# Two channel tiles of a 31-tap depthwise convolution: from VectorE/GpSimd taps to column-grouped fp32 products on TensorE

## The chip, the core and the metric

The kernel runs on one core of a Trainium2 chip. The metric is device time in microseconds of one execution; three executions of the kernel before took 2930.77, 2932.99 and 2934.18 us, median 2932.99 us. The engines are called PE (TensorE matmul), PEld (its weight loads), DVE (VectorE), ACT (ScalarE), POOL (GpSimd) and SP (SyncE, which here only issues DMAs). All arithmetic is fp32; the large products split each operand into a high part `wh`/`hh` and a low part `wl`/`hl` in the faster fp32r format and add three products.

## The reference

Two trunk layers over 512 latent tokens and 256 context tokens of width 1024. Each layer is half-step SwiGLU, a token mixer, half-step SwiGLU. The change lies in the mixer of the even (first) layer, which runs two head groups side by side: multi-head latent attention with 8 heads, and a Conformer convolution module over 512 channels:

```python
def conv_module(u, prm):
    u = u + prm["conv_glu_b"]
    a, g = jnp.split(u, 2, axis=-1)
    y = a * jax.nn.sigmoid(g)
    y = depthwise_conv(y, prm["conv_dw_w"], width 31, zero padding 15 on both sides) + prm["conv_dw_b"]
    y = layer_norm(y, prm["conv_ln_g"], prm["conv_ln_b"])
    return jax.nn.silu(y)
```

Latent and context tokens are convolved separately. The results of both head groups are concatenated and multiplied by `w_out`.

## The kernel before, in words

Features lie on the 128 partitions and tokens along the free axis, so the 512 convolution channels are four tiles c = 0..3 of 128 channels. `conv_unit(c)` makes one tile's gated input: two products of the mixer's input with 128 columns of weights (8 row tiles, three split products each, for 512 and 256 tokens), a sigmoid on ACT, and two DVE instructions that add the bias, multiply and write `yb[c]`: one row of 813 numbers per channel, with zeros ahead, between and behind latent and context. Before each product, `unit` loads 128 x 1024 weights (SP queue), rounds them on ACT (`wh`, line 210) and takes the rest on DVE (`wl`, line 211); PE needs both, and the load buffer is free again only when DVE has made `wl`.

`conv_taps(c, lo, hi, pool)` applies taps to a row of 783 outputs `cv[c]`. Tap 0 is one ACT instruction (line 768). On DVE another tap is one fused multiply-add (line 774). On POOL it is two instructions, a product into a scratch row and an addition (lines 771 and 772). The division of the 4 x 31 taps is:

- tiles 0 and 2: 2 ACT taps and 60 DVE taps, handed over ahead of the attention;
- tile 1: 1 ACT tap and 30 POOL taps, and of tile 3 taps 0 to 7 (1 ACT, 7 POOL), handed over at the same place;
- tile 3, taps 8 to 11: POOL, inside the attention; taps 12 to 30: 19 DVE taps inside the attention, one per query tile at some of them.

`even_mixer` hands its work over in this order: first low-rank product `wA`; `conv_unit` 0 to 3; second low-rank product `wB` (a `sweep` over six token tiles); transposes of both low-rank results (`lora_t`, line 899, ACT high part in line 901, DVE low part through line 199); keys and values (`up_tile`), their norms; queries, their norms and rotation; the taps; attention (`flow`); the layer norm of the convolution (`conv_ln`); its activation (`conv_act`); the output product `mix_out`.

What sets the order: a planner goes through the handed-over instructions with a cost estimate of its own and writes down a fixed order for each engine, taking what is ready, earlier-handed first. So the taps, handed over late, fill holes that the planner sees on DVE and POOL from the moment `yb[c]` exists. On the chip each engine then runs its list strictly in that order. The attention is different: its instructions are pinned, that is, kept in the order written. `flow` has 48 items (8 heads x 6 query tiles); an item may carry extras, among them single taps (`TAPT`, `PTAPT`), quarter transposes of the next head's operands, and one of the 14 steps of `conv_ln`. Those steps begin at item `LN0` = 25 or later, when no tap is left.

Buffers: areas A0 to E3 are shared by name. A0 to A3 hold the residual stream until the mixer's input is made (it is saved to HBM and read back by `mix_out`), A3 then serves as POOL's scratch row, A0 to A2 later hold the keys. PSUM has three pairs of banks handed out in turn by `pd()` (names `pa`, `pb`), and two single banks (`p`).

Of the kernel before, what the change touches and what calls it, by code (L numbers as in the profile page):

```python
# [31 lines left out]
TAPS3 = 12  # L32
TAPS3E = 8
LN0 = 25
# [17 lines left out]
DT = (0, 0, 0, 0, 0, 0, 99, 0)  # L52
PT = (0, 0, 0, 0, 0, 0, 99, 0)
TAPT = (0, 2, 4, 5)
PTAPT = (0, 2, 4)
# [38 lines left out]
class Kern:  # L94
# [57 lines left out]
    # one of twenty areas A0..E3; a new tile takes over the area from the one before  # L152
# [4 lines left out]
    # n rows of width w, so many per area  # L157
# [23 lines left out]
    # two banks, from the three pairs in turn  # L181
# [52 lines left out]
    # r = 1 / sqrt(ss * inv_n + eps), one Newton step after the table's square root  # L234
# [19 lines left out]
    # per-token 1/rms of the accumulated squares, the same on all partitions  # L254
# [36 lines left out]
    # four column chunks of 256 go to four column groups; a last product with a  # L291
    # selector brings both vectors to the feature layout
# [29 lines left out]
    # the same on the vector engine: half of the columns, two row tiles per unit  # L322
    def mod_dve(self):
        nc = self.nc
        self.mod_fin(1)
        L, m = self.mq[0]
        nv = self.mv(L, m)
        hh, kk = self.mk // 4, self.mk % 4
        u = self.mt().rearrange("p (a n) -> p a n", a=2)
        c0 = m * 1024 + hh * 512  # L330
        nc.sync.dma_start(u, self.I[f"modw{L}"][kk * 256:(kk + 1) * 256, c0:c0 + 512].rearrange("(a p) n -> p a n", p=128))
        if kk == 0:
            self.macc = [self.t768()[:, :512] for _ in range(nv)]
        for a in range(2):
            for v in range(nv):
                sc = self.sT[:, kk * 2 + a, v:v + 1]
                if kk == 0 and a == 0:
                    nc.vector.tensor_scalar(self.macc[v], u[:, a, :], sc, None, op0=ALU.mult)
                else:
                    self.stt(self.macc[v], u[:, a, :], sc, self.macc[v], ALU.mult, ALU.add)  # L340
        self.mk += 1
        if kk < 3:
            return
        if hh:
            self.mk = 0
            self.mq.pop(0)
        acc = self.macc

        r = slice(0, 64 * nv)
        st = {}  # L350

        # sums over the rows, one column group per vector and quarter
        def sums():
            p = self.p1()[:, 0:256]
            for v in range(nv):
                for q in range(2):
                    g = 64 * v + 32 * q
                    nc.tensor.matmul(p[g:g + 32, :], self.ones[:, 0:32], acc[v][:, q * 256:(q + 1) * 256], start=True, stop=True, tile_position=(0, g))  # L358
# [13 lines left out]

        self.mfin += [sums, fin]
# [6 lines left out]
    # vectors that a part is needed for  # L380
# [3 lines left out]
    # one step in the background; no half is begun that the slots left can't end  # L384
# [36 lines left out]
    # operand of an FFN: x * g * (1 + scale), split; the rms factor comes after the product  # L421
# [23 lines left out]
    # the shift's columns on their own, both parts side by side  # L445
# [131 lines left out]
    # modulated input of a mixer, split, in slots B and C  # L577
# [15 lines left out]
    # tokens x columns product, k outer; returns one PSUM area per token tile  # L593
# [26 lines left out]
    # natural-layout product with resident split operands (lora up-projections)  # L620
# [8 lines left out]
    # keep an engine's order as traced  # L629
# [66 lines left out]
    # values of two query tiles side by side in the columns of the array  # L696
# [14 lines left out]
    # the two halves to the rows of head h  # L711
# [14 lines left out]
    def rope_tables(self, gname, cname, sname, n, h):  # L726
        # g1*cos, g2*sin, g1*sin, g2*cos
# [31 lines left out]
    # taps lo..hi of one channel tile; latent and context share one row with zeros between  # L759
    def conv_taps(self, c, lo, hi, pool, pin=lambda i: i):  # L760
# [4 lines left out]
        for w in range(lo, hi):  # L765
            yw = y[:, w:w + CW]
            if w == 0:
                pin(nc.scalar.activation(cv, yw, AF.Identity, bias=self.col("dwb")[:, c:c + 1], scale=dw[:, 0:1]))
            elif pool:
                t = self.ctmp or self.mt()[:, :CW]  # L770
                pin(nc.gpsimd.tensor_scalar(t, yw, dw[:, w:w + 1], 1.0, op0=ALU.mult, op1=ALU.mult))
                pin(nc.gpsimd.tensor_tensor(cv, cv, t, op=ALU.add))
            else:
                pin(nc.vector.scalar_tensor_tensor(cv, yw, dw[:, w:w + 1], cv, op0=ALU.mult, op1=ALU.add))  # L774

    # layer norm over the channels, in steps; what a step returns follows one step later
# [57 lines left out]
    def even_mixer(self):  # L834
# [7 lines left out]
        self.ctmp = self.area("A3")[:, :CW]  # L842
# [4 lines left out]
        # lora parts  # L847
# [12 lines left out]
        tq = [(c, w) for c in (0, 2) for w in range(31)]  # L860
        pq = [(1, w) for w in range(31)] + [(3, w) for w in range(TAPS3E)]
        p3 = [(3, w) for w in range(TAPS3E, TAPS3)]
        d3 = [(3, w) for w in range(TAPS3, 31)]

        def taps(i):
            for q, n in ((pq, PT[i]), (tq, DT[i])):
                for c, w in q[:n]:
                    self.conv_taps(c, w, w + 1, q is pq)
                del q[:n]

        self.conv_unit(0)
        self.conv_unit(1)
        taps(0)
        self.conv_unit(2)
        taps(1)
        self.conv_unit(3)
        taps(2)
# [9 lines left out]
        taps(3)  # L887
        taps(4)
        # transposed lora activations, gains applied on the way
# [14 lines left out]
        # keys and values  # L904
# [25 lines left out]
        taps(5)  # L930
        # shared rotary part of the keys
# [13 lines left out]
        # a quarter of head h's transposed operands: three token tiles of K or of Q  # L945
# [19 lines left out]
        # queries  # L965
# [37 lines left out]
        taps(6)  # L1003
        tq += d3
        # attention
        self.ctmp = None
# [18 lines left out]
        def mk(h, t):  # L1025
# [22 lines left out]
            if t in TAPT and tq and (tq[0][0] != 3 or not p3):  # L1048
                c, w = tq.pop(0)
                ex.append(lambda: self.conv_taps(c, w, w + 1, False, self.pin))  # L1050
            if t in PTAPT and p3:
                w3 = p3.pop(0)[1]
                ex.append(lambda: self.conv_taps(3, w3, w3 + 1, True, self.pin))
# [4 lines left out]
            if h * 6 + t >= LN0 and ln and not tq and not p3:  # L1058
# [7 lines left out]
        for c, w in tq:  # L1066
            self.conv_taps(c, w, w + 1, False)
# [8 lines left out]
    def rope_q(self, x, T, nh):  # L1076
        # x [128, nh, 64] of one latent token tile, in place
# [12 lines left out]
    def odd_mixer(self):  # L1090
# [19 lines left out]
        # grouped-query part  # L1110
# [22 lines left out]
        # neighbourhood part  # L1133
# [18 lines left out]
        # split keys and queries, on the way to their transposes  # L1152
# [35 lines left out]
        # GQA keys [kh;kh], [kl;kl] and queries [qh;ql], once half of the sweep is done  # L1188
# [24 lines left out]
        # attention  # L1213
# [3 lines left out]
        # heads of the neighbourhood part: [kh;kl], [qh;qh], [ql;ql], two sets in turn  # L1217
# [165 lines left out]
    def build(self):  # L1383
# [20 lines left out]
        for L in range(2):  # L1404
# [15 lines left out]
            # the latent half of the norm and of the mixer's input runs under the context's products  # L1420
# [56 lines left out]
def _units(w):  # L1477
    # [1024, 128 * n] -> [n, 128, 8 * 128]: unit n holds its columns for the 8 row tiles
# [19 lines left out]
def _rows(w):  # L1498
    # [1024, n] -> [128, 8 * n]
# [3 lines left out]
def _pp(v):  # L1503
    # [128 * n] -> [128, n]
# [18 lines left out]
def _perm(a):  # L1523
    # latent tokens: row-major to column-major on the grid
# [25 lines left out]
def layout(a):  # L1550
# [42 lines left out]
    put("dwb", _pp(a["l0_conv_dw_b"]))  # L1593
    put("lng", _pp(a["l0_conv_ln_g"]))
# [58 lines left out]
```

## Time and profile before

| | |
|---|---|
| three runs | 2930.77, 2932.99, 2934.18 us |
| profiled execution | span 2929.3 us from first to last instruction; no time of its own is given beside the span, which is 3.7 us under the runs' median |
| busy over the span | PE 2812.6, PEld 2436.2, DVE 1708.6, ACT 855.1, POOL 460.0 us |
| granted TensorE clock | mean 0.982 |
| first and last DVE tap (line 774) | starts at 675.1 and 944.9 us, 79 of them |
| POOL taps (lines 771, 772) | 41 pairs, from 690.4 to about 879 us |
| first attention score product (line 1035) | 864.1 us |
| first `mix_out` product | 991.8 us |

How to read it: times of the trace count from the span's start. A wait is idle time of an engine, with the instruction that ended it. A row of the timeline gives start, length, engine, line, operation and operands; "x7" means seven instructions in a row. PE instructions are recorded with overlapping, modelled ends, so the distance between starts is the better measure of PE's pace. An fp32 product appears as two PE instructions, an fp32r product as one. The stage table gives, for stretches of the span, each engine's busy time, PE's granted clock (1.00 is full speed) and DMA use.

### The profile page before, as it was taken

What the parts mean: (1) busy time and instruction counts of PE and PEld (TensorE: products, weight loads), DVE (VectorE), ACT (ScalarE), POOL (GpSimd) and SP (SyncE); (2) the same over time, 40 slices, a digit from 0 to 9 for tenths busy, and PEclk for the clock granted to TensorE, in tenths of its full rate; (3) what the DMA queues carried; (4) which work ended last, traced back from release to release, by engine and by line L of the source; (5) the groups of instructions that cost most, each with busy time, mean ns of one, the idle gap of its engine ahead of it and who ended that gap; (6) DMA issues with size and microseconds to landing.
All of it is one profiled execution on the core that took longest, in us unless ns stands there. A gap on an engine that the chain in (4) does not pass through costs nothing.

```text
span 2929.3 us, 41724 instructions
## 1 busy us (share of the span) xinstructions
PE 2812.6 (96%) x17276; PEld 2436.2 (83%) x17276; DVE 1708.6 (58%) x2709; ACT 855.1 (29%) x1281; POOL 460.0 (16%) x435
## 2 busy tenths in 40 slices
PE   8999999998479899999999999999999999999999
PEld 5888888887467788888888888888888888898998
DVE  2665666688987676656545533333336779643443
ACT  3211212242156522112122221121224257332221
POOL 1000000035943330000000300000011256300000
PEclk9999999999789999999999999999999999999999
DMA  6433343431010223333433111112124200222232
GB/s 219 129 122 124 120 139 116 127 124 46 31 42 2 72 87 120 118 116 116 140 126 102 59 63 66 59 60 69 59 86 126 65 12 30 87 94 94 88 97 90
DMA packets 93740, 266.62 MB, mean 91 GB/s; under 512 B 8816, under 2 KB 9968, under 8 KB 93552
## 3 DMA queue, kind: packets, MB, share of 16 engines
q1 hardware_dynamic: 86512, 247.89, 26.6%
q10 hardware_dynamic: 5376, 10.83, 1.2%
q0 software_dynamic: 1664, 5.24, 0.5%
q8 instruction: 136, 2.23, 0.3%
q14 instruction: 52, 0.43, 0.0%
HBM read 255.80 MB, written 7.34 MB: 90 GB/s over the span
## 4 chain that ended last, share of the span: by engine, by line
PE 88%; DVE 7%; ACT 2%; issue 1%; DMA 1%; POOL 1%; ACTq 0%; SPq 0%; DVEq 0%; POOLq 0%
PE pa L190 53%; PE pb L190 26%; DVE D L774 3%; PE p L706 2%; PE pb L659 2%; DVE wl L211 1%; PE pa L1035 1%; PE pa L1263 1%; PE p L358 1%; ACT t L661 1%; PE p L193 0%; DMA r<-in_modw 0%; DVE sm L672 0%; PE p L279 0%; DVE C L199 0%
## 5 line engine op out<-in xcount | busy, mean ns | idle before, releaser
L210 ACT CAST wh<-r 128x1024 fp32r<-128x1024 f32 (+3 forms) x334 | 340.6, 1020 | 1517.8 <-PE pa L190 776.1
L190 PE MATMUL pa<-B,wh 128*128 128x512 f32 (+1 forms) x1984 | 492.8, 330 | 10.9 <-DVE D L199 8.6
L190 PE MATMUL pa<-B,wl 128*128 128x512 f32 (+1 forms) x1984 | 487.5, 327 | 0.0
L190 PE MATMUL pa<-C,wh 128*128 128x512 f32 (+1 forms) x1984 | 487.0, 327 | 0.3 <-DVE C L428 0.3
L211 DVE TENSOR_TENSOR wl<-r,wh 128x1024 fp32r<-128x1024 f32 (+3 forms) x334 | 410.7, 1230 | 39.8 <-ACT wh L210 31.0
L190 PEld LDWEIGHTS pa<-B,wh 128*128 128x128 f32 x1984 | 308.6, 190 | 50.9 <-issue 15.8
L190 PEld LDWEIGHTS pa<-C,wh 128*128 128x128 f32 x1984 | 307.9, 190 | 35.7 <-issue 0.7
L190 PEld LDWEIGHTS pa<-B,wl 128*128 128x128 f32 x1984 | 307.7, 190 | 34.1 <-issue 0.5
L199 DVE SCALAR_TENSOR_TENSOR t<-m,sT,t 128x512 f32<-128x512 f32 x392 | 275.7, 752 | 3.9 <-DMA m<-in_modw 2.8
L190 PE MATMUL pa<-E,wh 128*128 128x512 f32 (+1 forms) x919 | 257.7, 347 | 1.3 <-POOL E L215 1.3
L517 DVE COPY sm<-pa 128x2 f32<-128x2 f32 x116 | 18.4, 159 | 395.7 <-PE pa L190 395.1
L190 PE MATMUL pb<-B,wh 128*128 128x512 f32 (+1 forms) x960 | 236.5, 328 | 0.0
L190 PE MATMUL pb<-B,wl 128*128 128x512 f32 (+1 forms) x960 | 234.0, 325 | 0.0
L190 PE MATMUL pb<-C,wh 128*128 128x512 f32 (+1 forms) x960 | 233.5, 324 | 0.0
L190 PE MATMUL pa<-D,wh 128*128 128x512 f32 (+1 forms) x777 | 204.4, 339 | 0.1
L190 PE MATMUL pa<-D,wl 128*128 128x256 f32 (+1 forms) x737 | 196.3, 339 | 0.0
L1416 POOL DMA_DIRECT2D xs<-A x24 | 13.5, 562 | 1089.0 <-DVE A L199 1087.3
L190 PEld LDWEIGHTS pa<-E,wh 128*128 128x128 f32 x919 | 148.2, 188 | 24.3 <-POOL E L215 1.7
L190 PEld LDWEIGHTS pb<-B,wh 128*128 128x128 f32 x960 | 148.6, 189 | 19.6 <-issue 4.2
L190 PEld LDWEIGHTS pb<-C,wh 128*128 128x128 f32 x960 | 148.2, 189 | 16.2
L190 PEld LDWEIGHTS pb<-B,wl 128*128 128x128 f32 x960 | 148.2, 189 | 15.8
L199 DVE SCALAR_TENSOR_TENSOR A<-pa,hg,A 128x256 f32<-128x256 f32 (+1 forms) x95 | 54.9, 614 | 172.1 <-PE pa L190 172.0
(329 smaller groups left out, 4470.3 us busy)
## 6 DMA issues: line engine op xcount, KB each, us to landing
m<-in_modw SPq DMA_DIRECT2D x140, 512.0 KB, 3.7
r<-in_win0a SPq DMA_DIRECT2D x44, 512.0 KB, 4.2
r<-in_win0b SPq DMA_DIRECT2D x44, 512.0 KB, 3.5
r<-in_win1a SPq DMA_DIRECT2D x44, 512.0 KB, 3.4
r<-in_win1b SPq DMA_DIRECT2D x44, 512.0 KB, 3.4
r<-in_wodd SPq DMA_DIRECT2D x18, 512.0 KB, 3.7
r<-in_wout0a SPq DMA_DIRECT2D x20, 448.0 KB, 3.5
r<-in_wout1a SPq DMA_DIRECT2D x20, 448.0 KB, 3.4
```

The costliest lines, as they stand in the source:

```text
L190: self.nc.tensor.matmul(out, l.bitcast(F32R), r.bitcast(F32R), start=st, stop=sp)
L199: self.nc.vector.scalar_tensor_tensor(o, a, s, b, op0=op0, op1=op1)
L210: pin(self.nc.scalar.copy(hi, r))
L211: pin(self.nc.vector.tensor_tensor(lo, r, hi.bitcast(F32), op=ALU.subtract))
L358: nc.tensor.matmul(p[g:g + 32, :], self.ones[:, 0:32], acc[v][:, q * 256:(q + 1) * 256], start=True, stop=True, tile_position=(0, g))
L517: nc.vector.tensor_copy(w2[:, o:o + 2], p[:, so:so + 2])
L659: pin(nc.tensor.transpose(pt[:, ks], P[:, ks], self.col("ident")))
L661: pin(nc.scalar.copy(PT[:, :m], pt[:, :m]))
L706: self.pin(self.nc.tensor.matmul(self.po[i * 64:(i + 1) * 64, col:col + 128], v, self.PTs[i][:, kt * 128:(kt + 1) * 128], start=(kt == 0), ...
L774: pin(nc.vector.scalar_tensor_tensor(cv, yw, dw[:, w:w + 1], cv, op0=ALU.mult, op1=ALU.add))
L1035: self.pin(nc.tensor.matmul(s[:, o:o + b - a], q[:, ts].bitcast(F32R), k[:, a:b].bitcast(F32R), start=j == 0, stop=j == 2))
L1263: self.pin(nc.tensor.matmul(s[:, a:b], q.bitcast(F32R), k[:, a:b].bitcast(F32R), start=j == 0, stop=j == 1))
```

## The change

Tiles 1 and 3 are computed on TensorE. `conv_fan` copies the finished row `yb[c]` to four operands Y[0..3], one for each 32 channels: Y[g] has the 32 channels four times on its 128 partitions, copy s shifted by s tokens. That is 16 SBUF-to-SBUF DMAs of 32 partitions x about 811 fp32 numbers (about 104 KB) per tile, alternately on the SP and the ACT queue. `conv_mm` then multiplies Y[g] by a 128 x 32 weight block with the taps 4j..4j+3 on its diagonals, for j = 0..7 (tap 31 is zero), once for the 512 latent and once for the 256 context outputs. The four g go to four column groups of the array (`tile_position`), plain fp32; that makes 64 products per tile. Two ACT instructions add the bias and write `cv[c]`. The weight blocks are laid out on the host (`wdw`, 512 KB per tile), loaded by SP. Y lies in areas A0 to A3, whose last columns are zeroed by four small POOL instructions.

Tiles 0 and 2 keep their 2 ACT and 60 DVE taps, handed over at the same place. POOL has no tap, the attention has none, and the 14 layer-norm steps begin at item 8 instead of 25 or later. Comments are removed too, which shifts line numbers by a few.

```diff
-TAPS3 = 12
-TAPS3E = 8
-LN0 = 25
+PEC = (1, 3)
+LN0 = 8
...
+    def conv_fan(self, c, Y):
+        nc = self.nc
+        y = self.yb[c]
+        n = CW + 28
+        for s in range(4):
+            for g in range(4):
+                m = min(n, YW - s)
+                e = (nc.sync, nc.scalar)[(s + g) % 2]
+                e.dma_start(Y[g][32 * s:32 * s + 32, 0:m], y[32 * g:32 * g + 32, s:s + m])
+
+    def conv_mm(self, c, Y):
+        nc = self.nc
+        wd = self.mt()
+        nc.sync.dma_start(wd, self.I["wdw"][PEC.index(c)])
+        p = self.pd()
+        for j in range(8):
+            for a, b, o in LNREG:
+                for g in range(4):
+                    nc.tensor.matmul(p[32 * g:32 * g + 32, a:b], wd[:, j * 128 + 32 * g:j * 128 + 32 * g + 32],
+                                     Y[g][:, o + 4 * j:o + 4 * j + b - a], start=j == 0, stop=j == 7, tile_position=(0, 32 * g))
+        for a, b, o in LNREG:
+            nc.scalar.activation(self.cv[c][:, o:o + b - a], p[:, a:b], AF.Identity, bias=self.col("dwb")[:, c:c + 1])
...
-        self.ctmp = self.area("A3")[:, :CW]
+        Y = [self.area(n)[:, :CW + 28] for n in ("A0", "A1", "A2", "A3")]
+        for a in Y:
+            nc.gpsimd.memset(a[96:128, CW + 27:CW + 28], 0.0)
...
         self.conv_unit(0)
         self.conv_unit(1)
-        taps(0)
+        self.conv_fan(1, Y)
         self.conv_unit(2)
-        taps(1)
+        self.conv_mm(1, Y)
         self.conv_unit(3)
-        taps(2)
+        self.conv_fan(3, Y)
         pt = self.sweep(self.I["wB"], 0, 384, 2, range(6))
...
-        taps(3)
-        taps(4)
+        self.conv_mm(3, Y)
...
-        taps(6)
-        tq += d3
-        self.ctmp = None
+        for c in (0, 2):
+            self.conv_taps(c, 0, 31)
...
-            if t in TAPT and tq and (tq[0][0] != 3 or not p3):
-                c, w = tq.pop(0)
-                ex.append(lambda: self.conv_taps(c, w, w + 1, False, self.pin))
-            if t in PTAPT and p3:
-                w3 = p3.pop(0)[1]
-                ex.append(lambda: self.conv_taps(3, w3, w3 + 1, True, self.pin))
...
-            if h * 6 + t >= LN0 and ln and not tq and not p3:
+            if h * 6 + t >= LN0 and ln:
                 ex.append(ln.pop(0))
```

More of the change, by code (lines that the diff above doesn't have):

```diff
@@ L51 @@
 ROPE_E = lambda nc, i: nc.vector
[L52 to L55, printed above, removed]
 LR, LT, LV = 2, 4, 7
@@ L757, in conv_unit, with conv_taps @@
         self.stt(self.yb[c][:, 15 + C1:15 + C1 + NC], pp[0][:, 512:768], gb[:, c:c + 1], sg[:, 512:768], ALU.add, ALU.mult)
-    def conv_taps(self, c, lo, hi, pool, pin=lambda i: i):
+    def conv_fan(self, c, Y):
[19 more added lines that the diff above has]
+            nc.scalar.activation(self.cv[c][:, o:o + b - a], p[:, a:b], AF.Identity, bias=self.col("dwb")[:, c:c + 1])
+    def conv_taps(self, c, lo, hi, pin=lambda i: i):
         nc = self.nc
@@ L768, in conv_taps @@
                 pin(nc.scalar.activation(cv, yw, AF.Identity, bias=self.col("dwb")[:, c:c + 1], scale=dw[:, 0:1]))
[L769 to L772, printed above, removed]
             else:
@@ L859, in even_mixer @@
             self.pcopy(natA[t], natA[t], rA[:, 2 * t:2 * t + 1])
[L860 to L869, printed above, removed]
         self.conv_unit(0)
         self.conv_unit(1)
-        taps(0)
+        self.conv_fan(1, Y)
         self.conv_unit(2)
-        taps(1)
+        self.conv_mm(1, Y)
         self.conv_unit(3)
-        taps(2)
+        self.conv_fan(3, Y)
         pt = self.sweep(self.I["wB"], 0, 384, 2, range(6))
@@ L929, in even_mixer @@
         lora_t(natB, cqh, cql, 3, "qg")
-        taps(5)
         self.tt(kr, kr, v2(rA, 1).unsqueeze(2).broadcast_to((128, 6, 32)), ALU.mult)
@@ L1065, in even_mixer @@
         self.flow([mk(h, t) for h in range(8) for t in range(6)], self.I["wo0"], PRE)
-        for c, w in tq:
-            self.conv_taps(c, w, w + 1, False)
         for f in ln:
@@ L1593, in layout @@
     put("dwb", _pp(a["l0_conv_dw_b"]))
+    wd = np.zeros((len(PEC), 4, 32, 8, 4, 32), np.float32)
+    dw = np.concatenate([a["l0_conv_dw_w"], np.zeros((1, 512), np.float32)]).reshape(8, 4, 4, 4, 32)
+    for i, c in enumerate(PEC):
+        for k in range(32):
+            wd[i, :, k, :, :, k] = dw[:, :, c, :, k].transpose(1, 0, 2)
+    r["wdw"] = wd.reshape(len(PEC), 128, 1024)
     put("lng", _pp(a["l0_conv_ln_g"]))
```

## The prediction

> **What bounds the kernel now.** I read the page first, to see which engine sets the time and where it does not.
>
> ```profile
> PE 2812.6 (96%) x17276; PEld 2436.2 (83%) x17276; DVE 1708.6 (58%) x2709; ACT 855.1 (29%) x1281; POOL 460.0 (16%) x435
> ...
> PE   8999999998479899999999999999999999999999
> ...
> DVE  2665666688987676656545533333336779643443
> ...
> POOL 1000000035943330000000300000011256300000
> PEclk9999999999789999999999999999999999999999
> ```
>
> One slice is 73.2 us. PE is full everywhere but in the tenth to thirteenth slices, about 660 to 950 us, the even mixer; there DVE is at 8 to 9 tenths and POOL at 5 and 9. So PE bounds the kernel, and only in this hole can less work elsewhere shorten it. Next the stage table, cut where PE's idle stretches begin and end (busy us of PE, PEld, DVE, ACT, POOL; then the granted clock), and PE's waits from 690 to 864 us.
>
> ```profile
> 690.00:711.00 21.00, 21.00 (x122) 18.34 (x121) 20.68 (x14) 3.73 (x4) 19.65 (x11) 1.00 0.14 38
> 711.00:720.00 9.00, 0.53 (x4) 0.20 (x2) 8.93 (x7) 0.00 (x0) 8.55 (x6) 0.67 0.04 5
> 720.00:735.00 15.00, 14.27 (x68) 12.30 (x68) 14.96 (x9) 3.40 (x4) 14.27 (x9) 0.86 0.11 27
> 735.00:751.00 16.00, 0.00 (x0) 0.00 (x0) 15.86 (x11) 0.00 (x0) 15.27 (x9) 0.59 0.06 21
> 751.00:780.00 29.00, 26.01 (x137) 24.82 (x137) 28.64 (x17) 11.04 (x24) 27.63 (x16) 0.91 0.16 50
> 780.00:801.00 21.00, 0.00 (x0) 0.00 (x0) 20.75 (x13) 1.72 (x4) 20.09 (x11) 0.50 0.06 19
> 801.00:824.00 23.00, 21.30 (x89) 16.55 (x89) 17.73 (x26) 15.68 (x31) 21.64 (x16) 0.89 0.06 18
> ...
> 852.00:864.00 12.00, 1.05 (x3) 0.50 (x4) 11.79 (x25) 4.88 (x8) 0.00 (x0) 0.58 0.26 87
> sum 174.00, PE 105.67 PEld 91.07 DVE 164.07 ACT 52.33 POOL 136.22; mean PE 10.57 PEld 9.11 DVE 16.41 ACT 5.23 POOL 13.62
> ```
>
> ```profile
> PE pa L190 <- DVE D L199: 25.6, 2, 16.9
> PE pa L190 <- DVE C L199: 21.6, 1, 21.6
> PE pa L190 <- DVE B L199: 6.6, 1, 6.6
> PE pb L954 <- DVE C L196: 5.7, 1, 5.7
> PE pb L954 <- DVE E L196: 4.0, 1, 4.0
> ...
> PE pb L954 <- DVE C L960: 1.4, 1, 1.4
> ```
>
> PE is idle for 68 of these 174 us, nearly all of it waiting for DVE. The cause is in the DVE list, before and after POOL begins its taps (first row of POOL, then rows of DVE):
>
> ```profile
> 690.44 1.65 POOL L771 TENSOR_SCALAR A<-D,small 128x783 f32<-128x783 f32 x1 [26.73 <-DVE D L199]
> ...
> 680.41 7.45 DVE L774 SCALAR_TENSOR_TENSOR D<-D,small,D 128x783 f32<-128x783 f32 x7
> 687.77 1.22 DVE L211 TENSOR_TENSOR wl<-r,wh 128x1024 fp32r<-128x1024 f32 x1
> ...
> 700.59 2.59 DVE L211 TENSOR_TENSOR wl<-r,wh 128x1024 fp32r<-128x1024 f32 x1
> 703.11 13.34 DVE L774 SCALAR_TENSOR_TENSOR D<-D,small,D 128x783 f32<-128x783 f32 x7
> ...
> 800.35 1.00 DVE L199 SCALAR_TENSOR_TENSOR C<-pb,small,B 128x768 fp32r<-128x768 f32 x1
> ```
>
> Alone, seven taps take 7.45 us (1.06 each) and a weight rest 1.22; beside POOL's taps the same seven take 13.34 (1.91 each) and the rest 2.59. A weight product's DVE work stands behind seven taps in the fixed list, so one round takes 8.7 us before and 15.9 after POOL begins, and PE, which uses a weight unit in half a `conv_unit`, runs dry.
>
> **The change part by part.** *POOL's 41 tap pairs go.* DVE returns to 1.06 us a tap. Two counts from the stage table: the taps alone before 690 us (DVE busy, count), then what touches a weight rest after it (PE, PEld, DVE; DVE writes seven):
>
> ```profile
> 660.00:690.00 30.00, 11.37 (x11) 1.00 0.24 70
> ```
>
> ```profile
> 690.00:804.00 114.00, 33.28 (x108) 19.46 (x108) 15.68 (x7) 0.77 0.10 30
> ```
>
> The 49 of 60 taps still to run at 690 us cost 52 us instead of the 92 that 1.91 each gives. The waits for DVE D (25.6) go whole. Of the wait for DVE C (21.6, the low part of the first transposes, queued behind taps) the 1.0 us of the instruction itself stays: 20.6 gone. Of the wait for DVE B (6.6, POOL's last taps lie under it) I take half, 3.3, because its DVE work remains. The waits from 852 us on (11.1 us, queries' norms with no POOL work beside them) stay. After each long wait PE also restarts at a lower granted clock: 0.86 over 15 us, 0.91 over 29 and 0.89 over 23 make 7.2 us of lost pace; some of that lies on idle time, so I count 5.5. Sum of what goes: 25.6 + 20.6 + 3.3 + 5.5 = 55.0 us. It would be 68 + 7 at the most, and nothing if DVE stays late.
>
> *The 60 DVE taps stay*, hidden only if PE has more to do than DVE. For PE's pace:
>
> ```profile
> 614.50 0.64 PE L358 MATMUL p<-t,ones 128*32 128x256 f32 x8
> 946.03 3.60 PE L785 MATMUL p<-D,ones 128*128 128x512 f32 x8
> 952.21 2.00 PE L785 MATMUL p<-D,ones 128*128 128x256 f32 x8 [0.86 <-DVE D L790]
> 652.46 0.61 PE L190 MATMUL pa<-B,wh 128*128 128x512 f32 x2
> ...
> 669.36 0.51 PE L190 MATMUL pb<-B,wh 128*128 128x512 f32 x2
> ```
>
> The last two rows are the first products of `conv_unit` 0 and 1: 16.9 us a unit. From 690 us PE has 13 us of unit 2, 16.9 of unit 3, about 27 of the `wB` sweep (the 29-us stretch holds most of it) and the new products: some 82 us. DVE has 52 of taps, seven weight rests of 1.2 and a few gate and norm instructions: under 70 us. PE covers it with 12 us to spare; without that cover each microsecond counts.
>
> *The 2 x 64 grouped products come.* Line 358 is the nearest row: four fp32 products of 128 rows x 32 columns x 256, in four column groups, 0.64 us for all four, the gaps to its neighbours not counted. Line 785 is a full fp32 product: 3.60 / 4 = 0.90 us for 512 columns, 2.00 / 4 = 0.50 for 256. Four groups thus cost little more than one full product. At best a set of four costs one: 8 x (0.90 + 0.50) x 2 tiles = 22.4 us. With the 0.14 us that line 358 pays on top, for both sizes, 26.9. I take the middle, 25.0. If the groups ran one after the other it would be four times 22.4, 89.6 us; line 358 speaks against that, since its four would then take 2.0. All of it lies on PE's path. The 4 ACT evictions lie under the following sweep or transposes.
>
> The Trainium skill, "TensorEngine Tiling (Array Packing)", Theoretical Speedup, allows up to 4x for 32 columns, and "TensorE: Matmul & The Clock Gate", Measured speedup vs the span model, gives 2.38x for three column tiles of 512. If I carry that 79% over to four tiles, an estimate from that page, the products cost 28 us instead of 25, and the forecast would be 3 us later.
>
> *The fan-out comes:* 16 DMAs for each tile, eight on SP and eight on ACT.
>
> ```profile
> E<-D ACTq DMA_DIRECT2D x6, 128.0 KB, 2.2
> m<-in_modw SPq DMA_DIRECT2D x140, 512.0 KB, 3.7
> 2355.42 1.77 ACTq L1211 DMA_DIRECT2D E<-D  x3
> ```
>
> The first row is the nearest: copies from SBUF to SBUF on ACT's queue, 128 KB, landed after 2.2 us, and three in a row are issued in 1.77 us, 0.59 each. Eight issues and one landing make 6.9 us. By bytes, 16 x 104 KB at the pace of a 512 KB load in 3.7 us make 12 us. One after the other, 16 x 2.2 = 35. I take up to 12. The first gated row is there at 690.4 us (POOL's first tap waited for it), unit 2 keeps PE until 703: cover 13 us. The second comes some 4 us after unit 3 and has the sweep less that, about 22 us. So I cost the fan-out at nothing; in series it is late by 22 and 13 us. Each first DMA waits for DVE's gate instruction. Behind it stand, on SP, the next weight loads (two units are loaded ahead), and on ACT the high parts (line 210) and the PSUM copies. The 4.7 us of issues for each tile fit into ACT, which is busy 52 of 174 us. The two 512 KB loads of weight blocks (3.7 us each) wait for nothing new on SP; the four POOL zeroings run before, on an idle POOL. Keys reuse Y's areas, but only after PE itself has passed the second set.
>
> A rule that speaks against this: the Trainium skill, "SBUF — State Buffer", Door 1: The DMA port swizzle, says that 32 partitions reach half of the ports, 189 GB/s for 1 MiB, and that two such transfers do not add up. An estimate from that page is 1.66 MB / 189 GB/s = 8.8 us a tile; the cover would still hold it.
>
> *The attention loses 19 DVE taps, and its 14 norm steps start at item 8.*
>
> ```profile
> 880.00:945.00 65.00, 63.39 (x584) 53.22 (x583) 54.45 (x101) 47.36 (x101) 24.96 (x28) 1.00 0.01 1
> 945.00:990.00 45.00, 37.99 (x264) 29.14 (x266) 27.62 (x65) 27.60 (x56) 14.43 (x16) 0.93 0.25 77
> ```
>
> Beside the taps PE is busy 63.4 of 65 us, so taking them away yields at most 1.6. The steps now lie from 945 us on, where PE loses 7.0 of 45; three operand splits of `mix_out` lie there too, and ACT is late. Moved ahead, the steps meet the full part, where ACT is already busy 47 of 65, but no split. I take a gain of 4; the ends are 9 gained (1.6 and all 7) and 7 lost (the same waits paid once more).
>
> **Sum.** 55.0 - 25.0 + 4 = 34.0 us. The profile's 2929.3 us become 2895.3; the span is 3.7 us under the median of 2932.99, so the runs should give 2899.0.
>
> **The rivals.**
>
> *Fan-out or fixed lists are late* (no change at worst). The planner does not know the chip's DMA pace. Were the 16 DMAs in series, 22 + 13 = 35 us of new PE waits eat the gain: 2899 + 35 = 2934; half of that gives 2916. For it: 32-partition copies appear nowhere before, and they head two strict queues. Against it: 0.59 us an issue with three in flight, and PE could take unit 3 first.
>
> *The column groups do not overlap* (the other side). At its place, the two sets of 64, the price is 89.6 instead of 25.0: 2899 + 64.6 = 2964. It decides from 59 us on (25 + 34), that is 1.84 us for each of the 32 sets of four. For it: no row has 512 columns in groups, nor a long chain of accumulation. Against it: line 358, 0.64 us.
>
> *The attention pays for the early norm:* 7 lost instead of 4 gained, 2910. For it: PE is full there; against it: the splits are elsewhere.
>
> *Everything clears:* all 57 us of waits ahead of 852, 7.2 us of clock and 9 in the attention go, products at 22.4: 2932.99 - 50.8 = 2882.
>
> **How the numbers follow.** Forecast 0.66 (2899, itself 2888 to 2910); everything clears 0.10; attention pays 0.05; fan-out or lists late 0.14, half of it still faster, the rest split between no change and slower; groups in series 0.05. The range leaves out the series case and the worst of the late fan-out above, and a sliver below: 2880 to 2926. Changes within 0.2% (6 us) can't be told from none here. Faster: 0.66 + 0.10 + 0.05 + 0.07 = 0.88; same 0.05; slower 0.07.
>
> **What would show it.** Two marks of before, the first full scores and the first `mix_out` products:
>
> ```profile
> 864.13 3.93 PE L1035 MATMUL pa<-B,C 96*128 96x512 f32 x12
> ...
> 991.83 0.95 PE L190 MATMUL pa<-E,wh 128*128 128x512 f32 x4
> ```
>
> DVE taps all at 1.0 to 1.1 us and 60 of them; no POOL work between 690 and 830; PE's waits for DVE D and C gone; clock 1.00 from 690 to the transposes; the new products as 256 PE instructions in some 25 us; the first score at about 834 instead of 864 us and the first `mix_out` product at about 958 instead of 992. The fan-out step is wrong if PE waits for a DMA ahead of a set; the group step, if a set of four takes over a microsecond on average; the attention step, if PE's idle time over the stretch that answers to 880 to 990 us is not below the present 8.6. The whole is wrong if DVE still makes PE wait after 690 us with taps at 1.06.

## The result, and the profile after

The changed kernel takes 2900.14 us (median of four runs, 2898.59 to 2902.06); the kernel before takes 2932.01 us (four runs, 2930.77 to 2934.18). The ratio is 0.9893, 95% interval 0.9879 to 0.9907. The forecast was 2899.0 us, so the sum is right to 1.1 us; two of its terms are not.

The page of the changed kernel (busy time and the 40 slices, now 72.4 us each) shows the hole of the tenth to thirteenth slices smaller. GpSimd is silent in the tenth and eleventh; what it does in the next ones is the attention's own work, from 828 us on:

```profile
PE 2823.3 (97%) x17532; PEld 2439.1 (84%) x17532; DVE 1629.4 (56%) x2690; ACT 855.6 (30%) x1283; POOL 316.3 (11%) x357
...
PE   8999999999978999999999999999999999999999
...
DVE  3665666678665576665456533332337689644443
...
POOL 1000000030022320000001200000021256300000
PEclk9999999999989999999999999999999999999999
```

The stage table from the first copies to the attention (columns as in the prediction): TensorE loses 1.7 of the first 54.5 us, at full clock, where in the kernel before it stood still from 711 to 720 us and from 735 to 751. Of the 15.9 us of idle time that are left, 14.2 lie behind the last tap.

```profile
690.00:744.50 54.50, 52.83 (x368) 42.16 (x367) 53.32 (x56) 9.17 (x11) 0.00 (x0) 1.00 0.36 88
744.50:822.00 77.50, 63.25 (x410) 52.68 (x409) 47.79 (x116) 43.54 (x88) 0.00 (x0) 0.95 0.16 49
```

TensorE's waits from 690 to 822 us: the three long ones of before (25.6, 21.6 and 6.6 us) are down to 1.7, 0.6 and 1.1; the queries' waits are there unchanged.

```profile
PE pb L959 <- DVE C L191: 5.7, 1, 5.7
PE pb L959 <- DVE E L191: 4.0, 1, 4.0
PE pa L185 <- DVE D L194: 1.7, 1, 1.7
...
PE pa L185 <- DVE B L194: 1.1, 1, 1.1
...
PE pa L185 <- DVE C L194: 0.6, 1, 0.6
```

VectorE's timeline: taps cost 1.00 to 1.07 us each all the way, and the last of the 60 ends at 744.5 us.

```profile
704.40 18.09 DVE L790 SCALAR_TENSOR_TENSOR D<-D,small,D 128x783 f32<-128x783 f32 x18
...
732.82 11.73 DVE L790 SCALAR_TENSOR_TENSOR D<-D,small,D 128x783 f32<-128x783 f32 x11
```

TensorE's timeline: the two sets of products, then the two marks, first score and first output product.

```profile
700.16 10.56 PE L774 MATMUL pa<-A,m 128*32 128x512 f32 x128
...
755.03 10.73 PE L774 MATMUL pa<-A,m 128*32 128x512 f32 x128
...
822.18 2.06 PE L1039 MATMUL pa<-B,C 96*128 96x512 f32 x5
...
959.68 0.95 PE L185 MATMUL pa<-E,wh 128*128 128x512 f32 x4
```

The first mark moved from 864.13 to 822.18 us, the second from 991.83 to 959.68. The first product of `conv_unit` 0 starts at 649.6 us instead of 652.5, a drift of 2.9 us that is there ahead of all that was changed (profiled executions of kernels alike up to there begin this product between 649.2 and 653.5 us). So the mixer reaches the attention 39.1 us earlier (forecast: 30), but the stretch from the first mark to the second grew from 127.7 to 137.5 us: 9.8 lost, where 4 were to be gained.

The same stretch in the stage table and in TensorE's waits, before and then after:

```profile
864.10:991.80 127.70, 118.64 (x949) 96.66 (x948) 93.97 (x186) 88.51 (x183) 49.77 (x53) 0.96 0.10 32
```

```profile
PE pa L1035 <- ACT t L675: 2.3, 2, 1.3
PE p L954 <- DVE B L960: 2.1, 2, 2.0
PE p L269 <- POOL acc L798: 1.1, 1, 1.1
PE p L785 <- DVE D L790: 0.9, 1, 0.9
```

```profile
822.20:959.70 137.50, 120.23 (x951) 97.81 (x949) 77.30 (x170) 88.64 (x183) 41.06 (x49) 0.94 0.10 30
```

```profile
PE pa L1039 <- ACT t L670: 3.8, 4, 1.7
PE p L274 <- DVE C L965: 3.1, 1, 3.1
PE p L959 <- DVE C L965: 2.4, 2, 2.2
PE p L264 <- POOL acc L814: 2.1, 1, 2.1
PE p L959 <- DVE B L965: 1.5, 2, 1.1
PE p L801 <- DVE E L965: 1.3, 1, 1.3
```

VectorE has 17 us less to do there, and TensorE waits more. (The row of 5.7 us that the same view has in every version is left out: it ends at the first score.) Most of the new waits are for `p`, the two single PSUM banks: quarter transposes (line 959) and the norm's products (lines 801, 264, 274) take turns in what the products with the values (line 701) leave free of them, and each waits until the other's bank has been read. Waits on `p` make 11.1 us after and 4.9 before, each with two smaller rows of 0.2 to 0.5 us; 2.1 and 1.1 of these are another kind, line 264 waiting for GpSimd's sum of squares. So the banks have 5.2 of the 9.8 us and the sum of squares 1.0. Of the rest, 1.5 are longer waits of the scores for ACT, and 1.6 are more busy time (120.2 instead of 118.6 us, at a granted clock of 0.94 instead of 0.96).

### The profile page after: what moved, and what is told of

It is laid out like the page before. It is cut to its first block, busy times and chain, and to the rows that moved or that the text cites. A ratio compares the mean times of both kernels' runs of the same rounds, so it can differ in the third digit from the quotient of the medians.

```text
span 2897.4 us, 42215 instructions
## 1 busy us (share of the span) xinstructions
PE 2823.3 (97%) x17532; PEld 2439.1 (84%) x17532; DVE 1629.4 (56%) x2690; ACT 855.6 (30%) x1283; POOL 316.3 (11%) x357
## 4 chain that ended last, share of the span: by engine, by line
PE 65%; DVE 2%; ACT 2%; issue 1%; DMA 0%; POOL 0%; ACTq 0%; DVEq 0%; POOLq 0%
PE pa L185 39%; PE pb L185 19%; PE p L701 2%; PE pb L654 2%; PE pa L1259 1%; PE pa L1039 1%; ACT t L656 1%; DVE sm L667 0%; PE p L353 0%; PE p L274 0%; PE pa L1285 0%; PE p L188 0%; PE p L1247 0%; DVE wl L206 0%; DVE t L194 0%
## 5 line engine op out<-in xcount | busy, mean ns | idle before, releaser
L185 PE MATMUL pa<-B,wh 128*128 128x258 f32 (+2 forms) x1952 | 482.9, 329 | 1.6 <-ACT B L422 1.6
L185 PE MATMUL pa<-C,wh 128*128 128x258 f32 (+2 forms) x1952 | 478.1, 326 | 0.3 <-DVE C L423 0.3
L185 PE MATMUL pa<-B,wl 128*128 128x258 f32 (+2 forms) x1952 | 478.2, 326 | 0.0
L206 DVE TENSOR_TENSOR wl<-r,wh 128x1024 fp32r<-128x1024 f32 (+3 forms) x334 | 400.5, 1200 | 44.2 <-ACT wh L205 35.9
L185 PE MATMUL pb<-B,wh 128*128 128x512 f32 (+1 forms) x992 | 245.7, 329 | 0.0
L185 PE MATMUL pb<-B,wl 128*128 128x512 f32 (+1 forms) x992 | 242.5, 326 | 0.0
L185 PE MATMUL pb<-C,wh 128*128 128x512 f32 (+1 forms) x992 | 241.7, 325 | 0.0
L185 PEld LDWEIGHTS pb<-B,wh 128*128 128x128 f32 x992 | 153.6, 189 | 20.7 <-issue 4.8
L185 PEld LDWEIGHTS pa<-D,wh 128*128 128x128 f32 x800 | 124.8, 188 | 21.6 <-issue 3.7
```

The lines of the kernel that those rows point to most:

```text
L185: self.nc.tensor.matmul(out, l.bitcast(F32R), r.bitcast(F32R), start=st, stop=sp)
L206: pin(self.nc.vector.tensor_tensor(lo, r, hi.bitcast(F32), op=ALU.subtract))
```

## The experiments

**Where the 9.8 us of the attention went.** First theory: the norm's steps cost more because they now lie in the full part of the attention; a late start brings it back. The first edit starts them at item 36, which I took for their old place.

```diff
-LN0 = 8
+LN0 = 36
```

> The changed kernel with the norm steps back at item 36, where they began before; everything else as changed. Stretch from the first score product to the first product of mix_out: 127.7 us before, 137.5 after. Theory (the early norm steps cost the attention): the stretch comes back to 126 to 129 us and the time to 2889 to 2892. Rival (the attention is slower for another reason, the areas or the lists around it): the stretch stays at 135 or more, the time within 3 us of the changed kernel, 2900.

2897.19 us (ratio 0.9882 [0.9867, 0.9897]), stretch 132.2 us: about half, by neither account. "Late" alone isn't the cause. The second edit keeps the early start, from item 5, but runs steps only at the query tiles 0 and 5 of a head, where no quarter transpose is made (these run at tiles 1 to 4, for all heads but the last).

```diff
-            if h * 6 + t >= LN0 and ln:
+            if h * 6 + t >= 5 and t in (0, 5) and ln:
```

> The changed kernel with the norm steps only at query tiles 0 and 5 of each head, from item 5 on, where no quarter transposes of the next head are handed over; the 14 steps then end at item 42. Theory (the steps and the quarter transposes take turns at the one single PSUM bank that the values leave free, and that is what stalls PE): waits on line 965 from products of lines 801, 264, 274 and 959 fall from about 10 us to under 3, the stretch is 123 to 128 us, the time 2886 to 2891. Rival (the norm's own work on ACT and DVE is too much for the full part, wherever it is put): the stretch stays above 133 us, the time at 2896 or more.

2895.37 us (0.9873 [0.9858, 0.9888]), stretch 129.7 us. TensorE's waits in the stretch: those for `p` are down to 2.1 us in sum, and the rest is now a wait of the scores for their PSUM pair, which ACT's exponential holds.

```profile
PE pa L1039 <- ACT t L670: 7.3, 4, 2.2
...
PE p L959 <- DVE B L965: 1.3, 2, 1.1
```

So the place within the head matters. Read again with this, the code says at which items the kernel before ran its steps: with its 19 taps it came to item 35, so the two means fell on items 35 and 36 (tiles 5 and 0), the first later product on 41 (tile 5) and the rest on the last head, which has no quarter transposes: no product of the norm ever met one. In the changed kernel four do (items 8, 9, 14, 16); with a start at item 36 one mean does (item 37). The third edit is that start:

```diff
-LN0 = 8
+LN0 = 35
```

> The changed kernel with the layer norm's steps from item 35 on, the item from which they ran in the kernel before (its last tap inside the attention was in item 35). Theory (the attention stretch of the changed kernel is 9.8 us longer only because of the items that the 14 steps fall on): first score at 821 to 825 us, stretch from first score to first output product 126 to 130 us, time 2890 to 2895 us. Rival (the 19 taps taken out of the attention, or the earlier arrival at it, cost something of their own): stretch 131 us or more, 2896 us or more.

2893.33 us (0.9868 [0.9854, 0.9883]). The stretch is 127.7 us as before, and its waits are those of the kernel before:

```profile
825.80:953.50 127.70, 118.64 (x950) 96.67 (x949) 77.24 (x167) 88.58 (x183) 41.30 (x49) 0.96 0.10 32
```

```profile
PE pa L1039 <- ACT t L670: 2.3, 2, 1.3
PE p L959 <- DVE B L965: 2.1, 2, 2.0
...
PE p L264 <- POOL acc L814: 1.1, 1, 1.1
PE p L801 <- DVE D L806: 0.9, 1, 0.9
```

The whole loss is the items that the steps fall on. The 19 taps that left VectorE's list there are worth nothing: 77 us of VectorE work instead of 94, and TensorE's stretch is the same to a tenth. (In the runs the gain over the changed kernel is 6.8 us and not 9.8; the profiled execution begins `conv_unit` 0 at 651.8 us, 2.2 later than the changed kernel's, a drift that is not explained here. From the second set of products to the first score it takes 1.4 us longer, at a granted clock of 0.88 instead of 0.93. That leaves 9.8 - 2.2 - 1.4 = 6.2 us, and its span is 6.3 us shorter.)

**What the GpSimd taps cost.** The kernel before, with the 41 pairs left out:

```diff
             elif pool:
-                t = self.ctmp or self.mt()[:, :CW]
-                pin(nc.gpsimd.tensor_scalar(t, yw, dw[:, w:w + 1], 1.0, op0=ALU.mult, op1=ALU.mult))
-                pin(nc.gpsimd.tensor_tensor(cv, cv, t, op=ALU.add))
+                continue
```

> The kernel before with POOL's 41 tap pairs left out (30 taps of tile 1 and 11 of tile 3 are not computed), nothing put in their place. Theory (POOL's taps hold the memory port that DVE's taps need): the 60 DVE taps ahead of the attention take 1.02 to 1.08 us, PE's waits for the gate and low-part instructions fall from 47 us to under 5, the first score comes at about 802 us (before 864; the change gained 39 there and pays 21 for its products), the time is 2868 to 2880. Rival (DVE's fixed list is simply too long, whoever shares the port): taps stay at 1.6 us or PE still waits 30 us or more, the time stays above 2900.

2872.32 us (0.9797 [0.9783, 0.9812]). All 79 VectorE taps take 1.02 to 1.04 us. Of the waits from 688 to 805 us, these are the three that were long before, now with no product set to cover anything:

```profile
PE pa L190 <- DVE B L199: 1.1, 1, 1.1
PE pa L190 <- DVE C L199: 0.9, 1, 0.9
...
PE pa L190 <- DVE D L199: 0.6, 1, 0.6
```

The first score comes at 805.2 us, 59.0 earlier than before, 57.2 without the drift (`conv_unit` 0 at 650.7): that is what GpSimd's taps cost ahead of the attention. The stretch inside the attention stays at 127.7 us although four pairs are missing there.

The reverse: the changed kernel, with 30 pairs of GpSimd instructions of that size put in, their result used by nothing.

```diff
         self.conv_mm(1, Y)
+        Z = self.area("E3")
+        for w in range(30):
+            self.nc.gpsimd.tensor_scalar(Z[:, 0:CW], self.yb[1][:, 0:CW], self.col("dw")[:, w:w + 1], 1.0, op0=ALU.mult, op1=ALU.mult)
+            self.nc.gpsimd.tensor_tensor(Z[:, 0:CW], Z[:, 0:CW], self.yb[1][:, w:w + CW], op=ALU.add)
```

> The changed kernel with 30 pairs of GpSimd instructions of the old taps' size (a product and an addition, 128 x 783) put in after the first grouped products; their result is used by nothing. Theory (the stalls of before came from GpSimd slowing VectorE's taps, not from the number of taps): VectorE's taps beside them take 1.8 to 1.95 us instead of 1.05, the last tap ends 30 us or more later than 744 us, TensorE's waits for VectorE ahead of 830 us come back with 15 to 45 us in sum, time 2915 to 2945 us. Rival (the 41 taps' dependences and their place in the fixed lists made the stalls): taps stay near 1.05 us and the time within 2897 to 2904 us.

2951.16 us (1.0066 [1.0051, 1.0081]), beyond the expected 2945. GpSimd's two lines as groups (busy us, mean ns), a stretch of VectorE's taps, and TensorE's waits:

```profile
L886 POOL TENSOR_TENSOR E<-E,D 128x783 f32<-128x783 f32 x30 | 67.3, 2242 | 2.5
L885 POOL TENSOR_SCALAR E<-D,small 128x783 f32<-128x783 f32 x30 | 46.9, 1563 | 29.9 <-DVE D L194 27.0
```

```profile
689.52 21.07 DVE L790 SCALAR_TENSOR_TENSOR D<-D,small,D 128x783 f32<-128x783 f32 x11
...
717.64 36.08 DVE L790 SCALAR_TENSOR_TENSOR D<-D,small,D 128x783 f32<-128x783 f32 x18
```

```profile
PE pa L185 <- DVE D L194: 37.5, 2, 32.5
PE pa L185 <- DVE wl L206: 4.6, 1, 4.6
```

Taps cost 21.07 / 11 = 1.92 and 36.08 / 18 = 2.00 us again, though their inputs, their place in the list and their number are those of the changed kernel; no tap depends on the added work. So it is GpSimd running beside them, not their number, that makes VectorE late. The Trainium skill, "SBUF — State Buffer", Who interferes with whom, says that a VectorE instruction with two inputs in SBUF contends with a GpSimd instruction that reads SBUF, and that the later one then blocks; the tap has two such inputs, and 1.05 against 2.00 us agrees. Which of the two waits for which isn't visible here.

**What the products cost.** The column group as the outermost loop, so that neighbours share a group:

```diff
-        for j in range(8):
-            for a, b, o in LNREG:
-                for g in range(4):
+        for g in range(4):
+            for j in range(8):
+                for a, b, o in LNREG:
```

> The grouped products with the column group as the outermost loop: the same 2 x 64 products, but the 16 of one group follow one another, so neighbours never lie in different groups. Theory (four groups run side by side only because neighbours lie in different groups; that is why both sets took 21.3 us): the sets take about four times as long, 80 to 90 us, all of it on TensorE's path: 2955 to 2970 us, first score at about 880 us or later. Rival (the time of a 32-column product is small by itself, whatever its neighbours): sets stay at 21 to 25 us, 2898 to 2904 us. A value between the two would say that only part of the overlap comes from the order.

2955.09 us (1.0083 [1.0066, 1.0100]): slower than before. The two sets:

```profile
700.61 37.72 PE L774 MATMUL pa<-A,m 128*32 128x512 f32 x128
...
780.71 37.72 PE L774 MATMUL pa<-A,m 128*32 128x512 f32 x128
```

The same 2 x 128 instructions take 75.4 us instead of 21.3, 54.1 more, and the time grows by 55.0 us. Overlap of the four groups is what decides the sign of the change, and it hangs on the loop order. 37.72 / 10.56 = 3.57 of the 4 that the Trainium skill, "TensorEngine Tiling (Array Packing)", Theoretical Speedup, allows at most for 32 columns.

Each product twice (so the sums of these two tiles double):

```diff
-        for j in range(8):
+        for i in range(16):
+            j = i % 8
...
-                                     Y[g][:, o + 4 * j:o + 4 * j + b - a], start=j == 0, stop=j == 7, tile_position=(0, 32 * g))
+                                     Y[g][:, o + 4 * j:o + 4 * j + b - a], start=i == 0, stop=i == 15, tile_position=(0, 32 * g))
```

> The changed kernel with each set of grouped products done twice (the taps then count double), 256 more PE instructions in all. Theory (the sets lie on PE's path and the four groups run together): each set takes 21 us instead of 10.6, the time rises by 19 to 23 us to 2919 to 2923. Rival (PE waits for DVE's taps in that stretch anyway, so the products are free): the rise is under 8 us.

2925.12 us (0.9977 [0.9967, 0.9987]): 25.0 more than the changed kernel. Its sets take 20.90 and 21.06 us, together 20.7 more than the single ones, so the added products lie on TensorE's path. The other 4 us stand in the trace behind the sets: a wait for VectorE (line 194) is 1.4 us longer, and TensorE is busy 1.5 and 1.6 us longer ahead of and behind the second set, at granted clocks of 0.96 instead of 1.00 and 0.89 instead of 0.93.

**What the copies cost.** In the changed kernel's queues, the eight issues of the first set take 6.6 to 6.9 us (of the second, from 732.9 us on, 8.0 to 8.2), and a copy lands 2.7 to 5.6 us after its issue (median 3.7); the first set's products start at 700.16:

```profile
687.49 6.58 SPq L763 DMA_DIRECT2D A<-D  x8
...
687.49 6.85 ACTq L763 DMA_DIRECT2D A<-D  x8
```

By these rows the last copy of the first set lands at about 698 us (687.49 + 6.85 + 3.7), which leaves 2 us. (The expectation below takes 740.6 us, the last issue of the second set, for its first; from first issue to products that set has 22 us, as predicted.) Every copy issued twice:

```diff
-                e.dma_start(Y[g][32 * s:32 * s + 32, 0:m], y[32 * g:32 * g + 32, s:s + m])
+                for _ in range(2):
+                    e.dma_start(Y[g][32 * s:32 * s + 32, 0:m], y[32 * g:32 * g + 32, s:s + m])
```

> Every copy of the fan-out is issued twice in a row (same bytes to the same place): 32 instead of 16 copies a tile. Theory from the changed kernel's trace (first row set 687.5 to about 698 us, its products at 700.2, so some 2 us of cover; second set 740.6 to about 751, products at 755): a copy set of 15 to 20 us makes the first products wait 4 to 8 us for a DMA and the second ones 0 to 4, time 2904 to 2911 us. By the terms of the prediction (cover 13 and 22 us, 12 us a set) 24 us a set: 11 us late at the first and 2 at the second, 2913 us. Rival (the copies have ample cover): no wait for a DMA, 2898 to 2903 us.

2914.30 us (0.9942 [0.9927, 0.9957]), 14.2 more than the changed kernel, over the 4 to 11 expected from the trace and nearest to the prediction's own terms (2913). First TensorE's first set (with the wait ahead of it), then its wait for VectorE ahead of the sweep's first product, then an ACT row:

```profile
708.98 12.53 PE L775 MATMUL pa<-A,m 128*32 128x512 f32 x128 [4.79 <-issue]
745.70 0.44 PE L185 MATMUL pa<-wh,B 128*128 128x384 f32 x1 [4.18 <-DVE D L194]
```

```profile
704.50 0.90 ACT L748 ACTIVATE t<-pb,small 128x768 f32<-128x768 f32 x1 [15.53 <-DMA A<-D]
```

The view of line 764 puts the 4.8 us of the first row down to these copies. The set itself is 2.0 us longer, and the next wait for VectorE is 2.5 us longer. Three such terms make 9.3 us; with the drift of 3.9 us (`conv_unit` 0 at 653.5) they give 13.2 of the 14.9 us by which the first score is later (837.0). The ACT row was not expected: the next unit's sigmoid stood in ACT's list behind 14 copies that need 0.93 us each.

**One tile of products instead of two.** With GpSimd out of the way there may be room for tile 3 on VectorE. Two divisions, both with the norm from item 35: 11 of its VectorE taps ahead of the attention and 19 in it, or all 30 in it.

```diff
-PEC = (1, 3)
-LN0 = 8
+PEC = (1,)
+LN0 = 35
+TAPS3 = 12
+TAPT = (0, 2, 4, 5)
...
-        self.conv_fan(3, Y)
...
-        self.conv_mm(3, Y)
...
+        self.conv_taps(3, 0, TAPS3)
+        tq = [(3, w) for w in range(TAPS3, 31)]
...
+            if t in TAPT and tq:
+                c, w = tq.pop(0)
+                ex.append(lambda: self.conv_taps(c, w, w + 1, self.pin))
...
-            if h * 6 + t >= LN0 and ln:
+            if h * 6 + t >= LN0 and ln and not tq:
```

> Only channel tile 1 as grouped products; tile 3 on VectorE again: tap 0 on ACT and 11 taps handed over ahead of the attention, 19 inside it at the items' positions 0, 2, 4 and 5, norm steps from item 35, no tap on GpSimd. Theory (without GpSimd beside them taps cost 1.05 us and both places have room: some 20 us of VectorE idle ahead of the attention, 50 of 128 us in it): against the two-tile version with the norm from item 35 (2893.3 us) the second set of products, 10.7 us of TensorE, is saved and nothing lost, 2881 to 2886 us, attention stretch 126 to 130 us. Rival (the 11 early taps hold up the transposes or the norms of keys and queries, for which TensorE waits): waits for VectorE of 5 to 12 us come back, 2887 to 2895 us.

2888.06 us (0.9854 [0.9836, 0.9872]), stretch 127.4 us. The second division has `TAPS3 = 1` and a tap at all six tiles:

> As the run with one tile of products and 19 taps inside the attention, but all 30 VectorE taps of tile 3 inside it, one in each of the items 0 to 29, norm steps from item 35. Theory (VectorE has 94 of 128 us busy there with 19 taps, so 11 more fit): 2881 to 2887 us, stretch 126 to 131 us. Rival (taps at the items' positions 1 and 3, where VectorE also evicts the quarter transposes and reduces scores, are in TensorE's way): stretch 133 us or more, 2889 us or more.

2888.65 us (0.9853 [0.9837, 0.9869]), stretch 130.0 us; the first score is within a microsecond in both (819.6 and 819.9), so the 11 early taps cost nothing. Neither brings the 10.7 us of the set left out: against the two-tile version it is 5.3 and 4.7 us. The waits ahead of the attention in the first of the two show why in part:

```profile
PE pa L187 <- DVE st L244: 2.2, 1, 2.2
...
PE pb L187 <- ACT B L907: 1.6, 1, 1.6
```

The second set stood right between the sweep and the transposes, whose operands ACT and VectorE prepare; without it TensorE waits for them: with it, the first wait was not there and the second was 0.5 us. With a third wait, 0.8 us for ACT's line 891, that is 4.1 us which the two-tile version does not pay (2.2 + 1.1 + 0.8). In the trace that accounts for the rest: from `conv_unit` 0 to the first score the profiled execution is 6.3 us shorter, close to 10.7 - 4.1. The runs show a microsecond less (5.3), within their spread of 4 us. The first division is the fastest of the complete kernels here, with the second inside its interval: 12.1 us under the changed one, with intervals that don't meet, of which 6.8 belong to the norm's start.

## Why the prediction was right, and where it wasn't

**The removed waits (55.0 us): right.** Leaving out only the GpSimd taps moves the first score by 57.2 us. Waits for D, C and B keep 0.6, 0.9 and 1.1 us, so D did not quite go whole, C went as forecast, and B lost 5.5 instead of the half, 3.3, that I took. (49 taps at 1.91 us are 94 us and not the 92 of my working; no term rests on it.)

**"PE covers it with 12 us to spare": true but not needed.** I thought the 60 taps hidden only if the new products gave TensorE more to do. Without any product the waits stay just as small; seven taps at 1.05 us between weight rests are no hindrance by themselves.

**The added products (25.0 us): too dear.** They take 21.3 us, under my lower bound of 22.4: a set of four is 10.56 / 16 = 0.66 us on average over both sizes, where I had put one full product, 0.70, as the least. The full products of line 785 were not the floor I took them for. On the way to the first score they cost even less: 57.2 - 39.1 = 18.1 us (19.5 with the profiled execution of the start at item 35), in part because the second set, as the one-tile runs show, fills waits that are there without it. The estimate of 28 us from the Trainium skill, "TensorE: Matmul & The Clock Gate", Measured speedup vs the span model, was farther off: 79% of the ideal does not carry over to four groups in this loop, where 3.57 of 4, 89%, is reached. The other part of its miss is the price in series, which I took as 89.6 us and which is 75.4. The rival "column groups do not overlap" fell, but its mechanism is real: 75.4 us with another loop order, more than the 59 us from which I had it decide.

**The fan-out at nothing: right, with little to spare.** "Cover 13 us, up to 12" is 13 and about 10.5 in the trace. Issues were mis-sized: one copy per 0.86 us on ACT's queue (6.85 / 8), not 0.59; with a landing of 3.7 us instead of 2.2 that is 10.5 us where I had 6.9. Whether the issues or the bytes set the pace was not separated. The Trainium skill's port rule ("SBUF — State Buffer", Door 1: The DMA port swizzle) gave an estimate of 8.8 us a tile, below the 10.5 of these rows. Twice the copies cost 14.2 us where my terms give 13, but that is luck: TensorE waits 4.8 us for copies at the first set and not at all at the second, where I had 11 and 2; most of the rest are the longer set, the longer wait for VectorE and the drift.

**The attention (+4): this step failed.** Two readings in it were wrong. The 1.6 us that TensorE lost beside the taps did not come from the taps: without them the stretch is the same 127.7 us. And of the 7.0 us lost from 945 us on, only 1.9 went when the norm was moved ahead: the like 45 us of the changed kernel (second row below) still lose 5.1. The part ahead of them, where the steps met the quarter transposes in the two single banks, takes 74.8 us instead of 65.0 and loses 11.6 (first row) where the kernel before lost 1.6. Together that is 16.7 us of idle time, not below the 8.6 of before, which is the sign that I had named for a wrong step. I priced the move by how busy the engines were, and did not ask which PSUM buffer each step takes and at which items another user of it stands. The rival "attention pays for the early norm" had the sign, with 7 us for the measured 9.8.

```profile
838.10:912.90 74.80, 63.24 (x498) 50.25 (x497) 39.41 (x87) 45.14 (x95) 22.07 (x25) 0.93 0.05 15
912.90:957.90 45.00, 39.87 (x354) 32.87 (x353) 27.03 (x61) 30.53 (x65) 13.98 (x19) 1.00 0.18 54
```

**The sum.** In the trace: 39.1 gained ahead of the attention instead of 30.0, 9.8 lost in it instead of 4 gained, 2.9 of drift; -32.2 us at the second mark against a forecast of -34.0. The total came out by luck: an error of 9.1 us, one of 13.8 and the drift nearly cancel.

## What to carry to other kernels

Before a step is moved within an order written by hand, list the buffers that it takes and the places where another step takes them; a start at item 35 instead of 8 was worth 6.8 us with no other edit. Price work on GpSimd by what it does to VectorE beside it: 37 pairs ahead of the attention held TensorE up for 57 us. Check a forecast by marks inside the kernel and not by its total, since two wrong terms can add up to a right one.

## What was not expected of the hardware

- Four fp32 products of 128 x 32 in four column groups, 512 or 256 columns, average 0.66 us together when issued in turn; the same 16 per group one after the other take 37.72 / 64 = 0.59 us for each single one.
- VectorE's taps and GpSimd's instructions run at one common pace: taps at 1.92 to 2.01 us beside GpSimd instructions of 1.56 and 2.24, mean 1.90; those are means over rows, and single taps there last from 1.03 to 2.65 us. That looks like one tap per GpSimd instruction in turn, but single pairs were not followed.
- TensorE's granted clock also falls around waits of two to three us. In the changed kernel's attention a wait of 2.1 us ends at 864.5 us, with twelve one-column products behind it, and the clock is 0.50 from 866 to 868 us. Waits of 2.2 and 3.1 us end at 874.8 and 878.5; the clock is 1.00 up to 876 and 0.50 from 878 to 882. The 512-column product of the norm there (two instructions) takes twice the time that the kernel before shows for it at clock 1.00 (1.02 us, at 977.87). That the waits lower the clock is read from their order in time; no run changes a wait alone.

```profile
878.46 2.08 PE L274 MATMUL p<-m,ones 128*128 128x512 f32 x2 [3.12 <-DVE C L965]
```
